# Forming two sums of the up projection's weights by adding transfers instead of beforehand on VectorE

## The chip, the cores and the metric

The kernel runs on one core of a Trainium2 chip. The core has TensorE (PE in the profile; PEld is its weight load), VectorE (DVE), ScalarE (ACT), GpSimd (POOL), and SyncE (SP), which in this kernel issues all DMA transfers; sixteen DMA engines move the data. The metric is the device time of one execution in microseconds, taken as the median over runs. All data are float32, and the answer has to agree with the float32 reference.

## The reference

One layer of a decoder. A sequence of 1024 positions with 1024 features goes through two token mixers, whose results are gated and merged, and then through a gated MLP with a short convolution:

```python
h = rmsnorm(x, mix_norm)
q, k, v, su, sv, g_a, g_b = split(h @ w_in)
y_att = sliding_window_attention(q, k, v, ...)       # window 128
y_sgu = chunked_spatial_gating(su, sv, ...)          # chunks of 128
merged = sigmoid(g_a) * (y_att @ w_oa) + sigmoid(g_b) * (y_sgu @ w_ob)
x = x + merged @ w_out

z = rmsnorm(x, ffn_norm) @ w_up                      # 1024 -> 2 * 2816
zc = conv_b + sum(conv_w[t] * shifted(z, 2 - t) for t in range(3))
gate, val = split(zc)
x = x + (silu(gate) * val) @ w_down                  # 2816 -> 1024
```

The change concerns `@ w_up`, and with it the signs of a few intermediate sums in the gate projections (`g_a`, `g_b`).

## The kernel before

**Splitting.** TensorE multiplies in a reduced float32 format (fp32r). So each operand is split into a high part (a copy by ACT into fp32r) and a low part (the original minus the high part, by POOL or DVE), and each product is made of three matmuls: high with high, high with low, low with high. A weight operand can be used only when both parts are there.

**Seven products for eight.** The gate projections and the up projection compute two output tiles of 128 rows at once (a "pair") by a Strassen-Winograd scheme: the weights and the activations of a pair are cut into 2 x 2 blocks, sums of blocks are formed, and seven block products take the place of eight. In `Blocks.prod` each product is 4 x 3 = 12 matmuls of 128x512. The weight operands are A11 and A12 (one load, `sp`, held as `lp`), A21 and A22 (one load, `sq`), and four sums: S1 = A21 + A22, S2 = S1 - A11, S3 = A11 - A21, S4 = A12 - S2. On the activation side there are B11, B21, B22 and the sums T1 to T4. The results of the products are added up in PSUM and SBUF by DVE with the signs that belong to the scheme.

**The stages in time.** Attention and the first projections run until about 180 us; then the gates (8 pairs, `gate_pair`), the branches (16 jobs of `branch`, the products with `w_oa` and `w_ob`), eight output tiles (`out_tile`, the product with `w_out`), the up stage (22 pairs: `first_pair`, then `fast_pair` for n = 1 to 21), and the down products (`mms`, lines 1661 to 1674). The order of the instructions on each engine is written out by hand: an engine runs its own instructions in program order, and waits in that order.

**The sums S1 and S3 of the up stage.** They are made ahead of their use. `sums_step` runs 22 times, twice in each gate pair from the third on and then among the branches. Each time it issues the loads of A11, A21 and A22 for a later pair (`sums_load`, tile `ls`, two buffers), lets DVE form S3 and S1 (line 620), and stores both in DRAM (`sum`). In the up stage `load_s3` and `load_q` load them again, one pair ahead: S3 into the tile `s`, and S1 together with a plain load of A22 into `lq`.

**One pair of the up stage.** While TensorE runs the products of pair n in the order A11, S3, A12, S1, A22, S2, S4, the other engines prepare pair n+1. On POOL the order is: the low part of S3 (`split_s3`), the low part of A11/A12 (`split_p`, written `pl`), S2 and S4 (`sums_r`, written `lr`), the low part of S1/A22 (`split_q`, `ql`), and the low part of S2/S4 (`split_r`, `AX`). ACT makes the high parts just before. SP issues the stores of the previous pair's activations, then the load of `lp` for pair n+2, and, in the next pair, `lq` and `s`. DVE convolves and gates the previous pair and adds up the products.

**The transition.** The weights of pair 0 are loaded by `first_left`, during output tile 4, and split during the last output tiles. Pair 1 is loaded in `first_pair`. Because the norm of the MLP's input is known only when all output tiles are there, `first_pair` also computes it (`ssq_cols`, with a power on POOL at line 129, and `rms_rows`), and T2 and T4 are split late, on DVE (`late_split`).

Of the kernel before, what the change touches and what calls it, by code (L numbers as in the profile page):

```python
# [41 lines left out]
def body(ctx, tc, nc, a):  # L42
# [579 lines left out]

    def x_gain(r, ks):
        for k in ks:
            x = xr_raw[r][:, k, :]
            nc.scalar.activation(x, x, AF.Copy, scale=cp[:, 186 + 4 * r + k:187 + 4 * r + k])

    def x_sums(ks, first):
        for k in ks:
            x0 = xr_raw[0][:, k, :]  # L630
            if first:
                sub(nc.vector, x0[:, L], x0[:, H], x0[:, L])
            else:
                x1 = xr_raw[1][:, k, :]
                sub(nc.vector, x0[:, H], x1[:, H], x0[:, H])
                sub(nc.vector, x1[:, H], x1[:, H], x0[:, L])
                sub(nc.vector, x1[:, L], x1[:, L], x1[:, H])
# [181 lines left out]
    def v_end():  # L819
# [53 lines left out]
        sums_load()  # L873
# [11 lines left out]
        nc.vector.tensor_tensor(x7, x7, e, op=ALU.add)  # L885
        nc.vector.tensor_tensor(q.g1, x5, q.g1, op=ALU.add)
        nc.vector.tensor_tensor(q.v1, x7, q.v1, op=ALU.add)
        nc.vector.tensor_tensor(q.v0, q.u2, q.v0, op=ALU.add)
# [39 lines left out]
    class Left:  # L928
# [8 lines left out]
        def load_q(self):  # L937
            if self.i is None:
                self.q = wload(self.sq, "lq")
                return  # L940
            self.q = raw("lq")
            nc.sync.dma_start(self.q[:, 0:4], pools["sum"][self.i][:, 1])
            nc.sync.dma_start(self.q[:, 4:8], self.sq[:, 4:8])

        def load_s3(self):
            self.s3 = pools["wx"].tile([128, 4, 128], F, tag="s3", name=nm("s3"))
            nc.sync.dma_start(self.s3, pools["sum"][self.i][:, 0])
# [9 lines left out]
        def sum_s3(self):  # L957
            self.s3 = s3_pool.tile([128, 4, 128], F, tag="s3", name=nm("s3"))
            sub(nc.gpsimd, self.s3, self.p[:, 0:4], self.q[:, 0:4])

        def sum_f3(self):

            sub(nc.gpsimd, self.p[:, 0:4], self.q[:, 4:8], self.r[:, 0:4])
# [15 lines left out]
        def sum_s2(self):  # L979
            self.r = raw("lr")  # L980
            sub(nc.gpsimd, self.r[:, 0:4], self.q[:, 0:4], self.p[:, 0:4])

        def sum_s4(self):
            sub(nc.gpsimd, self.r[:, 4:8], self.p[:, 4:8], self.r[:, 0:4])
# [26 lines left out]
    class Blocks:  # L1011
# [23 lines left out]
        def sums(self, x1, x7, m4):  # L1035
# [3 lines left out]
            nc.vector.tensor_tensor(self.v0, self.u2, m4, op=ALU.add)  # L1039
            nc.vector.tensor_tensor(self.v1, x7, self.v1, op=ALU.add)  # L1040
# [8 lines left out]

    sums = {"load": 0, "make": 0}  # L1050

    def sums_load():

        i = sums["load"]
        if i < NPAIR:
            x = pools["ls"].tile([128, 3, 4, 128], F, tag="ls", name=nm("ls"), bufs=2)
            nc.sync.dma_start(x[:, 0], a["wup"][2 * i][:, 0:4])
            nc.sync.dma_start(x[:, 1:3], a["wup"][2 * i + 1].rearrange("p (b k) m -> p b k m", b=2))
            sums[i] = x
            sums["load"] += 1  # L1060

    def sums_step():

        i = sums["make"]
        if i < NPAIR:
            sums_load()
            x = sums.pop(i)
            sub(nc.vector, x[:, 0], x[:, 0], x[:, 1])
            sub(nc.vector, x[:, 1], x[:, 1], x[:, 2], ALU.add)
            t = pools["dr"].tile([128, 2, 4, 128], F, tag=f"sum{i}", name=f"sum{i}")  # L1070
            nc.sync.dma_start(t, x[:, 0:2])
            pools.setdefault("sum", {})[i] = t
            sums["make"] += 1

# [27 lines left out]
    def gate_pair(c, prev):  # L1102
# [16 lines left out]
        if c > 1:  # L1119
            sums_step()  # L1120
# [12 lines left out]
        nc.vector.tensor_tensor(x7, x7, q.g1, op=ALU.add)  # L1133
        if nx:
            nx.sums_r()
        if c > 1:
            sums_step()
# [58 lines left out]
    def branch(n):  # L1196
        br, c = B_ORDER[n]

        def main(w):
# [14 lines left out]
            if n % 2 == 0 or n in (5, 9):  # L1214
                sums_step()
# [50 lines left out]
    def out_tile(i):  # L1266
        d = D_ORDER[i]

        def main(w):
# [5 lines left out]
            if i == 5:  # L1275
                lefts[0].split_s3()
# [13 lines left out]
            if d < 4:  # L1290
                eng = nc.gpsimd if i < 6 else nc.vector
                right_split("B11", k, h[:, L], eng)
                sub(nc.vector, h[:, L], h[:, H], h[:, L])
                right_split("T1", k, h[:, L], eng)
            else:
                g = hs_[k]
                sub(nc.vector, g[:, H], h[:, H], g[:, H])
# [548 lines left out]
```

## Time and profile before

| | |
|---|---|
| median of 3 runs | 1193.8 us (1193.12 to 1194.03) |
| the profiled execution | 1193.8 us, of which 1192.1 us from the first to the last instruction |
| granted TensorE clock | 1.000 |
| TensorE matmul busy | 1180.0 us, 99% of the span |
| VectorE, ScalarE, GpSimd busy | 877.8, 541.8, 567.4 us |
| moved by DMA | 191.27 MB, 160 GB/s on the mean |

A row of a group or of a timeline names the line of the kernel, the engine, the operation, what is written and read by the program's names (`out<-in`), the shapes and the count; in a timeline the start and the length in us come first, and the idle time of the engine ahead of it, with what ended it, last. `SPq` marks SP's issue of a transfer; the issue rows give the size and the time from issue to landing. A busy TensorE in the profile is not TensorE at its peak, since the matmuls overlap and their ends are modelled, so the pace is read from the starts of the matmuls in the chain of waits. The idle time of an engine that nothing waits for costs nothing.

### The profile page before, as it was taken

Reading aid. Unit: us, or ns where it says so; the run is one execution under the profiler, and the core shown is the slowest. Engines: PE = TensorE matmul, PEld = TensorE weight load, DVE = VectorE, ACT = ScalarE, POOL = GpSimd, SP = SyncE. Lnnn points to the kernel's source line nnn. Section 1 sums busy time; section 2 is a strip of 40 time slices with the busy share of each in tenths; the row PEclk is TensorE's granted clock in tenths of the full one; section 3 lists DMA queues with packets and bytes.
Section 4 is the critical chain, followed back from the end, with each engine's and each line's share of the span. In section 5 each row is a group of like instructions: output and inputs, shape, how many; then the busy total and the mean of one; then the engine's idle time right before and its main releaser. Section 6 shows DMA issues by size and latency. Waiting matters only on the chain.

```text
span 1192.1 us, 15888 instructions
## 1 busy us (share of the span) xinstructions
PE 1180.0 (99%) x5890; PEld 1000.9 (84%) x5890; DVE 877.8 (74%) x1028; ACT 541.8 (45%) x832; POOL 567.4 (48%) x364
## 2 busy tenths in 40 slices
PE   8999999999999999999999999999999999999998
PEld 8989989988888888888888888888888888888887
DVE  7798975745638565668897788878788798865674
ACT  8555567644335222234544444444444445434331
POOL 2367685487768222343756575656657551000000
PEclk9999999999999999999999999999999999999999
DMA  7110133037786997342143342423333258966471
GB/s 272 35 54 19 54 136 130 5 130 260 245 315 212 347 327 278 125 165 100 54 142 108 104 143 98 148 91 124 108 131 124 89 209 290 373 230 194 151 233 67
DMA packets 79134, 191.27 MB, mean 160 GB/s; under 512 B 8913, under 2 KB 9169, under 8 KB 79057
## 3 DMA queue, kind: packets, MB, share of 16 engines
q1 hardware_dynamic: 79056, 190.26, 45.9%
q8 instruction: 46, 0.75, 0.3%
q14 instruction: 32, 0.25, 0.1%
HBM read 139.63 MB, written 50.59 MB: 160 GB/s over the span
## 4 chain that ended last, share of the span: by engine, by line
PE 89%; DVE 4%; POOL 1%; issue 1%; ACT 0%; POOLq 0%; DVEq 0%; ACTq 0%
PE pz L1028 48%; PE pd L1672 10%; PE pdy L1672 8%; PE px L93 2%; PE px L92 2%; PE po L93 2%; PE po L92 2%; PE po L91 2%; PE px L91 2%; PE pvs L91 1%; PE pvs L92 1%; PE pvs L93 1%; DVE ya L529 1%; PE pq L91 1%; PE pq L93 1%; PE pq L92 1%
## 5 line engine op out<-in xcount | busy, mean ns | idle before, releaser
L1028 PE MATMUL pz<-T,qh 128*128 128x512 f32 x472 | 145.6, 390 | 0.0
L988 POOL TENSOR_TENSOR pl<-lp,ph 128x1024 fp32r<-128x1024 f32 x30 | 72.5, 2418 | 83.5 <-ACT ph L87 83.3
L1028 PE MATMUL pz<-B,ph 128*128 128x512 f32 x352 | 109.1, 391 | 0.0
L1028 PEld LDWEIGHTS pz<-T,qh 128*128 128x128 f32 x472 | 88.5, 188 | 18.6 <-ACT u L879 0.3
L1028 PE MATMUL pz<-T,ql 128*128 128x512 f32 x236 | 91.8, 389 | 0.0
L108 POOL TENSOR_TENSOR wjl<-wj,wjh 128x512 fp32r<-128x512 f32 (+1 forms) x24 | 40.6, 1692 | 95.8 <-ACT wjh L87 95.8
L988 POOL TENSOR_TENSOR ql<-lq,qh 128x1024 fp32r<-128x1024 f32 x30 | 76.9, 2565 | 9.1 <-ACT qh L87 9.1
L1028 PEld LDWEIGHTS pz<-B,ph 128*128 128x128 f32 x352 | 65.3, 188 | 15.0 <-ACT x L1519 1.8
L1044 DVE TENSOR_TENSOR pz<-pz,rstd_b 128x1024 f32<-128x1024 f32 x60 | 73.9, 1232 | 4.2 <-ACT rstd_b L141 2.1
L988 POOL TENSOR_TENSOR s3l<-s,s3h 128x512 fp32r<-128x512 f32 x29 | 39.8, 1373 | 69.7 <-ACT s3h L87 69.7
L1028 PE MATMUL pz<-T,s3h 128*128 128x512 f32 x232 | 71.4, 389 | 0.0
L1028 PE MATMUL pz<-B,pl 128*128 128x512 f32 x176 | 68.6, 390 | 0.0
L1672 PE MATMUL pd<-bl,ah 128*128 128x512 f32 x176 | 68.5, 389 | 0.0
L1672 PE MATMUL pd<-bh,ah 128*128 128x512 f32 x176 | 68.5, 389 | 0.0
L1672 PE MATMUL pd<-bh,al 128*128 128x512 f32 x176 | 68.5, 389 | 0.0
L1028 PE MATMUL pz<-T,AX 128*128 128x512 f32 x264 | 63.4, 389 | 0.0
L1028 PE MATMUL pz<-B,AX 128*128 128x512 f32 x264 | 63.4, 389 | 0.0
L1028 PEld LDWEIGHTS pz<-T,AX 128*128 128x128 f32 x264 | 49.6, 188 | 10.3
L1028 PEld LDWEIGHTS pz<-B,AX 128*128 128x128 f32 x264 | 49.6, 188 | 10.3
L1378 DVE SCALAR_TENSOR_TENSOR tg<-pz,cp,tg 128x1023 f32<-128x1023 f32 (+1 forms) x44 | 56.2, 1278 | 0.8
L1378 DVE SCALAR_TENSOR_TENSOR tv<-pz,cp,tv 128x1023 f32<-128x1023 f32 (+1 forms) x44 | 56.2, 1277 | 0.8
L988 POOL TENSOR_TENSOR AX<-lr,AX 128x1024 fp32r<-128x1024 f32 x22 | 53.7, 2440 | 5.1 <-ACT AX L87 5.1
(342 smaller groups left out, 3511.8 us busy)
## 6 DMA issues: line engine op xcount, KB each, us to landing
ls<-wup SPq DMA_DIRECT2D x22, 512.0 KB, 5.3
sum<-ls SPq DMA_DIRECT2D x22, 512.0 KB, 5.3
lp<-wup SPq DMA_DIRECT2D x22, 512.0 KB, 3.6
ra<-wdown SPq DMA_DIRECT2D x44, 256.0 KB, 4.6
b<-T SPq DMA_DIRECT2D x44, 256.0 KB, 3.8
B<-tv SPq DMA_DIRECT2D x33, 256.0 KB, 2.0
T<-tt SPq DMA_DIRECT2D x33, 256.0 KB, 2.0
b<-B SPq DMA_DIRECT2D x33, 256.0 KB, 3.1
```

Of the source, the lines that this page charges most:

```text
L91: nc.tensor.matmul(out, wh, mh, start=first, stop=False, **kw)
L92: nc.tensor.matmul(out, wh, ml, start=False, stop=False, **kw)
L93: nc.tensor.matmul(out, wl, mh, start=False, stop=last, **kw)
L108: nc.gpsimd.tensor_tensor(l[:, :nk, :], r[:, :nk, :], h[:, :nk, :].bitcast(F), op=ALU.subtract)
L529: nc.vector.tensor_tensor(ya[r, 2 * half:2 * half + 2, b * 128:(b + 1) * 128], p[r, g], o[r], op=ALU.add)
L988: nc.gpsimd.tensor_tensor(l, r, h.bitcast(F), op=ALU.subtract)
L1028: nc.tensor.matmul(o, p[:, k, :], y[:, q, k, :], start=not more and k == 0 and j == 0, stop=k == 3 and j == 2, skip_group_check=True)
L1044: nc.vector.tensor_tensor(z, z, rstd_b, op=ALU.mult)
L1378: nc.vector.scalar_tensor_tensor(t[:, j:], p[:, 0:1024 - j], cw[:, ci, 2 - j:3 - j], t[:, j:], op0=ALU.mult, op1=ALU.add)
L1672: nc.tensor.matmul(o[d], p[:, k - k0, m], q[:, k - k0, :], start=new and k == 0 and j == 0, stop=k == HK - 1 and j == 2, skip_group_check= ...
```

## The change

S1 and S3 of the up stage are no longer made in gates and branches. Instead, three pairs ahead, plain loads bring A11's half of `sp` into a tile for S3 and the whole of `sq` (A21, A22) into a tile for S1/A22; both lie in a new buffer `lq` with two places, in memory that the output stage has used. A pair later POOL issues two transfers that add to what lies in SBUF: A21 onto A11, which gives S3, and A22 onto A21, which gives S1. The first two pairs use the old tiles (`raw` and `s3`), with the additions issued at output tile 5 for pair 0 and in `first_pair` for pair 1. An adding transfer can only add, so S3 is now A11 + A21, and with it S2 = S1 + A11 and S4 = A12 + S2: the blocks of the scheme get other signs, and the activation sums (`x_sums`, `out_tile`, `last_tile`) and the sums of the products (`v_end`, `gate_pair`, `Blocks.sums`, `first_pair`, `fast_pair`) follow. Where the negated sum of two blocks is needed, `neg_sum` makes it in one DVE instruction. In `first_pair` the split of S3 for pair 1 comes later, behind `ssq_cols`. Everything of `sums_load` and `sums_step` is removed, with the calls in `v_end`, `gate_pair` and `branch`.

```diff
+    def neg_sum(out, x, y):
+        nc.vector.scalar_tensor_tensor(out, x, -1.0, y, op0=ALU.mult, op1=ALU.subtract)
+        return out
...
         def load_q(self):
-            if self.i is None:
-                self.q = wload(self.sq, "lq")
-                return
-            self.q = raw("lq")
-            nc.sync.dma_start(self.q[:, 0:4], pools["sum"][self.i][:, 1])
-            nc.sync.dma_start(self.q[:, 4:8], self.sq[:, 4:8])
+            self.q = wload(self.sq, "lq")
 
         def load_s3(self):
             self.s3 = pools["wx"].tile([128, 4, 128], F, tag="s3", name=nm("s3"))
-            nc.sync.dma_start(self.s3, pools["sum"][self.i][:, 0])
+            nc.sync.dma_start(self.s3, self.sp[:, 0:4])
+
+        def load_ahead(self):
+            if "lq" not in pools:
+                pools["lq"] = U("lq", F, (128, 2, 2048))
+            x = pools["lq"][:, self.i % 2, :]
+            self.s3, self.q = (x[:, i:j].rearrange("p (k m) -> p k m", m=128) for i, j in ((0, 512), (512, 1536)))
+            nc.sync.dma_start(self.s3, self.sp[:, 0:4])
+            nc.sync.dma_start(self.q, self.sq)
+
+        def adds(self):
+            nc.gpsimd.dma_start(self.s3, self.sq[:, 0:4], accum_op=ALU.add)
+            nc.gpsimd.dma_start(self.q[:, 0:4], self.sq[:, 4:8], accum_op=ALU.add)
...
-    def sums_load():
-    def sums_step():
...
# gate_pair (twice), branch, v_end
-            sums_step()
-        sums_load()
...
# out_tile
             if i == 5:
+                lefts[0].adds()
+            if i == 6:
                 lefts[0].split_s3()
...
# first_pair
         nc.scalar.copy(x7, q.v0)
+        nx.adds()
         nx.split_p()
-        nx.split_s3()
...
         ratio = ssq_cols(pb)
+        nx.split_s3()
         nx.sums_r()
         nx.split_q()
         lefts[2].load_p()
+        lefts[2].load_ahead()
...
# fast_pair
         q.prod(q.g0, "A11", "B11")
-        if nx:
-            nx.load_q()
-            nx.load_s3()
-        else:
+        if rms:
+            lefts[3].load_ahead()
+        if not nx:
             hooks[2]()
...
             lefts[n].split_r(n)
+            nx.adds()
...
         if nx:
             nx.split_s3()
+        if n + 2 < NPAIR:
+            lefts[n + 2].adds()
...
             nx.split_q()
             nx.split_r(n + 1)
+            if n + 3 < NPAIR:
+                lefts[n + 3].load_ahead()
```

More of the change, by code (lines that the diff above doesn't have):

```diff
@@ L1431, in body @@
     U_ORDER = [i for j in range(HK) for i in (j, j + HK)]
-    lefts = [Left(a["wup"][2 * i], a["wup"][2 * i + 1], i) for i in U_ORDER]
+    lefts = [Left(a["wup"][2 * i], a["wup"][2 * i + 1], n) for n, i in enumerate(U_ORDER)]
     def first_left():
@@ L1543, in fast_pair @@
             nx.split_p()
-        nc.vector.tensor_tensor(x7, x7, q.g1, op=ALU.add)
+        sub(nc.vector, x7, x7, q.g1)
         if rms:
```

71 lines of the change are left out of this document (24 added, 47 removed).

## The prediction

> **What bounds the kernel now.** I read the page first: the engines' busy time, and the chain of work that ended last.
>
> ```profile
> span 1192.1 us, 15888 instructions
> ...
> PE 1180.0 (99%) x5890; PEld 1000.9 (84%) x5890; DVE 877.8 (74%) x1028; ACT 541.8 (45%) x832; POOL 567.4 (48%) x364
> ...
> PE 89%; DVE 4%; POOL 1%; issue 1%; ACT 0%; POOLq 0%; DVEq 0%; ACTq 0%
> ```
>
> TensorE is busy for 1180.0 of 1192.1 us and carries 89% of the chain, so the change can only act through gaps that it closes or opens on TensorE. A matmul's end is modelled in such a profile, so I checked that "busy" is dense. Next view: busy time by stage (gates 245 to 415, branches 415 to 480, output tiles and first pair to 580, the other pairs to 978, the down products to the end). Then, in one fence each, the waits of TensorE from 180 us on, and two long pieces of the chain of waits (start, length, what).
>
> ```profile
> 245.00:415.00 170.00, 170.00 (x752) 140.74 (x751) 96.52 (x100) 67.26 (x83) 119.75 (x68) 1.00 0.71 246
> 415.00:480.00 65.00, 65.00 (x288) 53.86 (x287) 38.56 (x37) 14.61 (x17) 15.86 (x12) 1.00 0.81 291
> 480.00:580.00 100.00, 100.00 (x457) 83.32 (x456) 75.91 (x68) 37.23 (x50) 45.20 (x24) 1.00 0.33 117
> 580.00:978.00 398.00, 398.00 (x1756) 328.37 (x1755) 329.38 (x315) 181.79 (x212) 241.65 (x123) 1.00 0.36 122
> 978.00:1192.00 214.00, 209.91 (x926) 173.13 (x924) 146.41 (x143) 82.16 (x92) 7.55 (x4) 1.00 0.64 220
> ```
>
> ```profile
> engine line waited for: us in total, times, longest us
> ```
>
> ```profile
> 580.39 397.86 PE pz L1028 x1752
> 978.24 29.92 PE pd L1672 x132
> ```
>
> The columns after each stretch are its length, then busy us and instruction count of TensorE matmul, weight load, DVE, ACT and POOL, the granted clock, the DMA share and GB/s. TensorE fills every stage that the change touches, at a clock of 1.00, and the list of its waits from 180 us on is empty under its header. The chain gives the pace: 397.86/1752 = 227.1 ns a matmul in the up pairs, 29.92/132 = 226.7 in the down products, though the DMA share is 0.36 in the first and 0.64 in the second; in the gates, at 0.71, it is 170.00/752 = 226.1 with one matmul counted at each edge. Lighter DMA traffic buys no faster matmuls. If all of the up pairs ran at 226.7, they would lose 1752 x 0.4 ns = 0.7 us, and the gates by the same reckoning 0.3 us: 1.0 us is nearly all that can be won behind 180 us. Ahead of 180 us the change touches no instruction but the order of operands in a few subtractions.
>
> **What goes away.** Each of the 22 pairs loses its preparation in gates and branches: two loads, two DVE additions, one store, and two loads of the stored sums.
>
> ```profile
> ls<-wup SPq DMA_DIRECT2D x22, 512.0 KB, 5.3
> sum<-ls SPq DMA_DIRECT2D x22, 512.0 KB, 5.3
> ...
> ls<-wup SPq DMA_DIRECT2D x22, 256.0 KB, 4.3
> s<-sum SPq DMA_DIRECT2D x22, 256.0 KB, 3.8
> ```
>
> ```profile
> L620 DVE TENSOR_TENSOR ls<-ls 128x512 f32<-128x512 f32 x44 | 44.5, 1010 | 9.4 <-DMA ls<-wup 8.6
> ```
>
> That is 44.5 us of DVE work (44 x 1010 ns) and 22 x (512 + 256 + 512) KB of traffic. DVE is busy for only 96.52 of 170 us and 38.56 of 65 us there, TensorE never waits for it, and so this is worth 0. SP loses 66 issues in those two stages; nothing waited behind them on TensorE's path: 0.
>
> **What is added, in the steady pairs.** In pair n, POOL issues two adding transfers (256 KB each) for pair n+2, between the low part of S3 and the low part of the A11/A12 weights of pair n+1. Each occupies POOL for a time i and lands L after its issue began; neither is in this trace. Here are POOL's instructions in one pair, and the matmul that first reads the low weights (pl).
>
> ```profile
> 699.89 1.30 POOL L988 TENSOR_TENSOR s3l<-s,s3h 128x512 fp32r<-128x512 f32 x1 [3.75 <-ACT s3h L87]
> 704.52 2.40 POOL L988 TENSOR_TENSOR pl<-lp,ph 128x1024 fp32r<-128x1024 f32 x1 [3.33 <-ACT ph L87]
> 706.88 1.74 POOL L620 TENSOR_TENSOR lr<-lq,lp 128x512 f32<-128x512 f32 x1
> 708.70 1.28 POOL L620 TENSOR_TENSOR lr<-lp,lr 128x512 f32<-128x512 f32 x1
> 709.94 2.40 POOL L988 TENSOR_TENSOR ql<-lq,qh 128x1024 fp32r<-128x1024 f32 x1
> 712.30 2.40 POOL L988 TENSOR_TENSOR AX<-lr,AX 128x1024 fp32r<-128x1024 f32 x1
> 717.97 1.29 POOL L988 TENSOR_TENSOR s3l<-s,s3h 128x512 fp32r<-128x512 f32 x1 [3.26 <-ACT s3h L87]
> ```
>
> ```profile
> 711.43 0.39 PE L1028 MATMUL pz<-B,pl 128*128 128x512 f32 x1
> ```
>
> POOL is idle for 3.33 us just where the two issues go, and pl, done at 704.52 + 2.40 = 706.92, is read at 711.43: 4.51 us of slack. So 2i may reach 3.33 + 4.51 = 7.84 us, i = 3.9 us, before TensorE sees it. Two lighter conditions: POOL's six instructions sum to 11.52 us of a pair of 84 x 0.227 = 19.07 us, so it keeps up while 2i is under 7.55 us; and an addition has about 16 us until the next pair's ACT copy of S3 (just ahead of 717.97) reads it. The plain loads that an addition waits for are issued when the buffer is free, at the end of ql (712.34): with SP's issue and 3.8 to 5.3 us to landing they are there at about 717 to 718, while POOL gets to the addition at 719.26. If they are late by 3 us, POOL's idle time absorbs it.
>
> For i the nearest rows are SP's issue of such a transfer (0.36 us, below) and POOL's longest instruction in this stage (2.81 us, below); for L, 3.8 us (s<-sum) and 5.3 us (ls<-wup). A gain is excluded as an end, since the operation is added. I take i = 1.30 us, POOL's own instruction on tiles of this size, and L = 4.3 us, the 256 KB load under busy DMA. At every one of these values the steady pairs cost 0. The DMA engines carry it too: a pair's transfers grow by the 512 KB of the additions, at a share of 0.36.
>
> **What is added, at the first pairs.** Here there is no pair of lead, and the chain is read row by row.
>
> ```profile
> 578.06 2.81 POOL L988 TENSOR_TENSOR ql<-lq,qh 128x1024 fp32r<-128x1024 f32 x1
> 582.53 2.40 POOL L988 TENSOR_TENSOR AX<-lr,AX 128x1024 fp32r<-128x1024 f32 x1 [1.67 <-ACT AX L87]
> ```
>
> ```profile
> 585.77 0.62 ACT L87 ACTIVATE s3h<-s 128x512 fp32r<-128x512 f32 x1
> ```
>
> ```profile
> 581.81 0.36 SPq L947 DMA_DIRECT2D s<-sum  x1
> ```
>
> ```profile
> 586.15 0.39 PE L1028 MATMUL pz<-T,ql 128*128 128x512 f32 x1
> ...
> 597.03 0.39 PE L1028 MATMUL pz<-B,pl 128*128 128x512 f32 x1
> ```
>
> Pair 1's S3 split moves behind the power of the norm (line 129), so POOL's ql ends later by up to one such instruction, 1.30 us alone and 1.74 as slow as its like beside DVE: 580.87 + 1.7 = 582.6. TensorE reads it at 586.15, 3.5 us of cover. POOL had 1.67 us of idle before AX, so AX still ends at about 585.0. There the additions for pair 2 are issued, and behind them in POOL's order stand S3's low part for pair 2, the additions for pair 3, and pl of pair 2. S3's low part waits for ACT's copy (0.62 us, plus about 0.1 to hand over), which now waits for the addition to land; ACT's x7 copy, ph and tanh are queued behind that copy. So pl ends at 585.0 + max(L + 0.73, 2i) + 1.30 + 2i + 2.40. It is read at 597.03, so TensorE stalls by L + 2i - 7.6 us where that is positive. With i = 1.30 and L = 4.3 the sum is 6.9: no stall, 0.7 us to spare. At the low ends (0.36, 3.8): 4.5, no stall. At the high ends (2.81, 5.3): 10.9, a stall of 3.3 us, once. The spare is thin, because loads of pairs 2 and 3 now follow each other at about 580 us (the old third issue was at 581.81); I charge 0.4 us for that, about half the spare.
>
> By the Trainium skill, page "DMA: Bandwidth & Descriptors", section on the anatomy of a DMA on the gpsimd path, such a transfer takes about 2.0 us plus bytes over 436 GB/s. With L by that estimate, 2.6 us, and the same i, L + 2i is 5.2 and the sum is 1193.8 us; no run here shows that queue yet.
>
> A second place is the T2 operand of pair 0, whose low part DVE makes just behind POOL's AX of pair 0.
>
> ```profile
> 554.18 0.75 DVE L1327 SCALAR_TENSOR_TENSOR h<-ac,cp,rstd_b 128x512 f32<-128x512 f32 x1
> ...
> 556.95 2.60 DVE L1327 SCALAR_TENSOR_TENSOR h<-ac,cp,rstd_b 128x512 f32<-128x512 f32 x1
> ...
> 563.36 4.12 DVE L1456 TENSOR_TENSOR T<-T2f,T 128x1024 fp32r<-128x1024 f32 x2 [0.36 <-ACT T L87]
> ```
>
> ```profile
> 568.42 1.76 PE L1028 MATMUL pz<-T,AX 128*128 128x512 f32 x7
> ```
>
> The same instruction takes 0.75 us alone and 2.60 us beside a POOL instruction: they block each other. At the pace of 0.75 us for half the size, each T2 instruction needs about 1.3 us, so of the 4.12 us the first part was a wait, and POOL let go at about 565.0. Pair 1's additions now follow there. T2 is complete at 567.48, and its second half is read from about 568.42 + 7 x 0.227 = 570.0. If the issues hold up its second instruction wholly, 2 x 2.81 us, T2 is there at 565.0 + 5.6 + 1.3 = 571.9, a stall of 1.9 us; if not at all, 0. I take 0, since an issue reads no tile. The additions for pair 0 (output tile 5) have more than one tile, 48 x 0.227 = 10.9 us, until they are read: 0. The replaced subtractions keep count and size: the form with a scalar took 0.75 us against about 0.7 of its neighbours, eight times beside TensorE's work: 0.
>
> **Sum.** The profiled execution took 1193.8 us (span 1192.1 and 1.7 around it), the same as the median of the runs. 1193.8 - 0 (gates, branches) + 0 (20 steady pairs) + 0.4 (pair 2) + 0 (T2) = 1194.2 us.
>
> **Rivals.** (a) Slower, by one mechanism: the wait of pair 2's first product for pl, behind the additions on POOL. It decides from L + 2i = 10.0 us, a stall of 2.4 us; at the high ends it is 3.3 us, 1197.1 us. For it: four issues and one landing stand in a row, and several 512 KB loads share the DMA then. Against: it needs both prices near their high ends.
>
> (b) Slower, DVE starving the issues. DVE is busy for 329.38 of 398 us; if each issue had to wait out one DVE instruction of about 1.3 us (as T2's), i would be 1.30 + 1.3 = 2.6 us, L 5.6 and L + 2i 10.8: 1197.0 us. Beyond i = 3.8 us POOL itself becomes the bound; at i = 4.5 that is 1.5 us in each of 20 pairs, 1224 us. The row that speaks for it is 2.60 against 0.75 us; against it, that pair of instructions both read tiles.
>
> The Trainium skill, page "SBUF — State Buffer", section on who interferes with whom, says that DVE's two-port copy forms keep POOL from writing descriptors, and that a tensor_tensor holds only the read side. By that rule (b) would not occur in the pairs, where DVE runs no such copies; the trace has no POOL issue to test it.
>
> (c) Faster: the relieved DVE, SP and DMA close TensorE's gaps. There is 1.0 us to be had by the pace above: 1192.8 us, still within the band. For 2.4 us there is no place behind 180 us.
>
> (d) The change doesn't do what it says: SP comes late, the loads aren't ahead, and additions wait on POOL. Up to 7.84 us per pair less 2i this costs 0: 1193.8 to 1194.2 us.
>
> **Chances.** 0.2% (2.4 us) is about what a measurement of this kernel can tell from no change. My forecast, with (c) inside its band, 0.61, and (d) 0.04: within. (a) 0.18, (b) 0.06, both places a little and something in the first pairs that I haven't seen 0.05: slower, 0.29. Faster 0.06, for a cause ahead of 180 us. The likeliest case alone spans 1192.8 to 1196.2. The range goes down to 1192.6 and up to 1198.4, the high ends of both places in part (3.3 of pair 2, 1.3 of the 1.9 of T2), and leaves out the faster case and the saturated part of (b).
>
> **What would show it.** Right: no wait of TensorE from 180 us on, 22 pairs of POOL issues, TensorE at 227 ns in all stages, DVE in gates and branches down by some 44 us and the span unchanged. Step by step: i from the spacing on POOL, L from issue to landing, pl of pair 2 done ahead of its first reader, T2's two instructions near 4.1 us. Wrong: an idle stretch of TensorE at the start of pair 2 or in pair 0's S2 product, or gaps at every pair, which would make i larger than 3.8 us.

## The result and the profile after

The changed kernel takes 1196.67 us (median of 10 runs, 1195.9 to 1197.14); the kernel before, on the same chip, takes 1193.11 us (10 runs). The ratio is 1.0029, 95% interval [1.0019, 1.0038]: slower by 0.3%, some 3.5 us. That is inside the range on record, but not where most of the chance lay: the forecast was "no difference", and there is one. Two executions in this document were slow, one of early_x1 at 1474.64 us with a granted clock of 0.752 and one of early_i4 at 1213.84 us; the ratios leave them out.

First the page of the changed kernel: span, busy times, the new queue, and the shares of the chain that ended last.

```profile
span 1195.1 us, 15765 instructions
...
PE 1181.0 (99%) x5890; PEld 1000.1 (84%) x5890; DVE 834.6 (70%) x984; ACT 540.9 (45%) x832; POOL 596.7 (50%) x408
...
q1 hardware_dynamic: 66384, 161.42, 39.0%
q0 software_dynamic: 6336, 11.54, 6.5%
...
PE 85%; DVE 5%; POOL 2%; ACT 1%; issue 1%; DMA 0%; POOLq 0%; ACTq 0%; DVEq 0%
```

Everything that was to become lighter did: VectorE lost 43 us, and 17 MB of traffic are gone. Now the stages (the columns as in the prediction), and TensorE's waits from 180 us on (engine and line, what it waited for, us in total, times, longest).

```profile
245.00:415.00 170.00, 170.00 (x751) 140.79 (x751) 64.38 (x70) 67.37 (x83) 112.42 (x68) 1.00 0.39 136
415.00:480.00 65.00, 65.00 (x289) 53.83 (x288) 28.16 (x23) 14.61 (x17) 15.77 (x12) 1.00 0.42 146
580.00:978.00 398.00, 396.12 (x1740) 325.10 (x1739) 326.96 (x312) 178.90 (x209) 274.01 (x162) 1.00 0.53 148
```

```profile
PE pz L1039 <- ACT x L1518: 1.7, 1, 1.7
```

In gates and branches VectorE does 32.1 + 10.4 us less, TensorE was full there before and is full now: worth nothing, as forecast. The whole difference is in the up stage, where 1740 matmuls fit into the 398 us that held 1756. And the list of waits, which was empty, has one row: a wait of 1.7 us for ACT's x7 copy (line 1518). 1.7 is only half of 3.5, so a second loss is hidden from this list. It shows in the distances between the starts of TensorE's matmuls: 2.10 us instead of 0.23 at 588.09 us (pair 1, product A22), then 0.48 and 0.34 us at 603.69 (pair 2, first of A12) and 0.40 and 0.34 us at 623.13 (pair 3, the same place). After that only two are over 0.40: 0.44 us in pair 10 and 0.41 us in pair 18, again at A12.

Where the first comes from is in ACT's timeline of the transition, before and after.

```profile
585.77 0.62 ACT L87 ACTIVATE s3h<-s 128x512 fp32r<-128x512 f32 x1
586.29 0.57 ACT L1533 COPY x<-pz 128x512 f32<-128x512 f32 x1
586.75 1.07 ACT L87 ACTIVATE ph<-lp 128x1024 fp32r<-128x1024 f32 x1
...
592.97 1.06 ACT L87 ACTIVATE AX<-lr 128x1024 fp32r<-128x1024 f32 x1 [0.74 <-POOL lr L620]
596.48 0.59 ACT L1038 COPY u<-pz 128x512 f32<-128x512 f32 x1 [2.45 <-DVE pz L1037]
```

```profile
589.03 0.63 ACT L87 ACTIVATE s3h<-lq 128x512 fp32r<-128x512 f32 x1 [3.27 <-DMA lq<-wup]
589.57 0.57 ACT L1518 COPY x<-pz 128x512 f32<-128x512 f32 x1
590.03 1.06 ACT L87 ACTIVATE ph<-lp 128x1024 fp32r<-128x1024 f32 x1
...
598.14 1.06 ACT L87 ACTIVATE AX<-lr 128x1024 fp32r<-128x1024 f32 x1 [4.01 <-POOL lr L620]
599.10 0.57 ACT L1049 COPY u<-pz 128x512 f32<-128x512 f32 x1
```

ACT's copy of S3 for pair 2 now waits 3.27 us for the landing of an adding transfer. Behind it on ACT stands the x7 copy, which empties the PSUM tile into which A22 of pair 1 goes on adding: that is TensorE's wait. Behind that stands ph, and at the end of this row of work the copy AX of S2 and S4, 5.17 us later than before, and right behind it the u copy. Before, the u copy waited 2.45 us for VectorE after AX was done; that spare is eaten, and the u copy is 2.62 us late. (These are differences of the times in the two traces. Just ahead of this stretch the changed kernel is 0.1 us early, so its lateness is 0.1 us more when it is counted from there, as in the table of the next section.) On POOL the same stretch shows what stands between ph and AX.

```profile
587.90 2.41 POOL L988 TENSOR_TENSOR pl<-lp,ph 128x1024 fp32r<-128x1024 f32 x1
590.27 1.28 POOL L620 TENSOR_TENSOR lr<-lq,lp 128x512 f32<-128x512 f32 x1
591.63 1.30 POOL L620 TENSOR_TENSOR lr<-lp,lr 128x512 f32<-128x512 f32 x1
```

```profile
584.77 0.90 POOL L957 DMA_DIRECT2D lq<-wup  x1
585.86 0.85 POOL L958 DMA_DIRECT2D lq<-wup  x1 [0.18 <-issue]
589.74 1.28 POOL L999 TENSOR_TENSOR s3l<-lq,s3h 128x512 fp32r<-128x512 f32 x1 [3.04 <-ACT s3h L87]
590.98 0.85 POOL L957 DMA_DIRECT2D lq<-wup  x1
591.56 1.16 POOL L958 DMA_DIRECT2D lq<-wup  x1
592.13 3.03 POOL L999 TENSOR_TENSOR pl<-lp,ph 128x1024 fp32r<-128x1024 f32 x1
594.51 1.89 POOL L620 TENSOR_TENSOR lr<-lq,lp 128x512 f32<-128x512 f32 x1
596.48 1.63 POOL L620 TENSOR_TENSOR lr<-lp,lr 128x512 f32<-128x512 f32 x1
```

The first fence is before, the second after. The low part of S3 starts 3.04 us late, two more issues follow it, and the second sum, which AX reads, ends at 598.11 instead of 592.93. Of these 5.2 us, 4.2 are there when pl starts; most of the rest is the two sums themselves, which take 1.89 and 1.63 us instead of 1.28 and 1.30.

From the u copy on, VectorE and ACT go through a fixed row of steps in each pair (u copy, taps, x1 copy, convolution, x7 copy, and so on), and TensorE's A12 needs the PSUM tile that the x1 copy empties. In both kernels the x1 copies of a pair and of the next but one lie 38.17 us apart, while TensorE needs 168 x 0.2267 = 38.09 us for two pairs. So this second chain doesn't catch up: it was 2.61 us late at pair 2 and is 2.62 us late at pair 8. The period alone doesn't tell whether the chain could go no faster or only follows TensorE; the experiments have to.

### The profile page after: what moved, and what is told of

The parts are those of the page before. It is cut to its first block, busy times and chain, and to the rows that moved or that the text cites. A ratio compares the mean times of both kernels' runs of the same rounds, so it can differ in the third digit from the quotient of the medians.

```text
span 1195.1 us, 15765 instructions
## 1 busy us (share of the span) xinstructions
PE 1181.0 (99%) x5890; PEld 1000.1 (84%) x5890; DVE 834.6 (70%) x984; ACT 540.9 (45%) x832; POOL 596.7 (50%) x408
## 3 DMA queue, kind: packets, MB, share of 16 engines
q1 hardware_dynamic: 66384, 161.42, 39.0%
q0 software_dynamic: 6336, 11.54, 6.5%
## 4 chain that ended last, share of the span: by engine, by line
PE 85%; DVE 5%; POOL 2%; ACT 1%; issue 1%; DMA 0%; POOLq 0%; ACTq 0%; DVEq 0%
PE pz L1039 43%; PE pd L1659 10%; PE pdy L1659 8%; PE px L92 2%; PE po L93 2%; PE po L92 2%; PE px L93 2%; PE px L91 2%; PE po L91 2%; PE pvs L92 1%; PE pvs L91 1%; PE pvs L93 1%; PE pu L93 1%; PE pu L91 1%; PE pu L92 1%
## 5 line engine op out<-in xcount | busy, mean ns | idle before, releaser
L999 POOL TENSOR_TENSOR s3l<-lq,s3h 128x512 fp32r<-128x512 f32 x20 | 25.9, 1296 | 63.0 <-ACT s3h L87 63.0
L87 ACT ACTIVATE AX<-lr 128x1024 fp32r<-128x1024 f32 x22 | 23.4, 1063 | 71.0 <-POOL lr L620 71.0
```

Of the source, the lines that this page charges most:

```text
L87: return nc.scalar.activation(dst, src, AF.Copy, scale=scale)
L999: nc.gpsimd.tensor_tensor(l, r, h.bitcast(F), op=ALU.subtract)
```

## The experiments

All runs are put into one table. The first numbers are the ratio to the kernel before with its 95% interval, and the difference of the medians to the kernel before in the same comparison. The last two are worked out from the one profiled execution: the stages ahead of the up stage vary by up to 1.5 us between executions, so both are taken from a common point, a matmul of pair 0 that starts 0.324 us ahead of the next in every trace (572.86 us in the kernel before), and compared with the same distance there. One is the end of the x1 copy of pair 2, the other the start of the last matmul.

| kernel | ratio, 95% interval | median, us | x1 copy, pair 2 | last matmul |
|---|---|---|---|---|
| the change | 1.0029 [1.0019, 1.0038] | +3.56 | +2.71 | +3.38 |
| no_add2 | 0.9991 [0.9982, 1.0000] | -1.01 | -0.74 | -0.55 |
| early | 1.0001 [0.9992, 1.0009] | -0.12 | -0.71 | +1.00 |
| x7_first | 1.0029 [1.0019, 1.0038] | +3.15 | +3.15 | +4.13 |
| adds3_late | 1.0014 [1.0006, 1.0023] | +1.43 | +1.59 | +2.35 |
| both_gates | 1.0012 [1.0004, 1.0021] | +1.78 | +1.40 | +2.01 |
| act_delay | 1.0031 [1.0020, 1.0043] | +3.91 | +0.03 | +4.07 |
| act_delay3 | 1.0014 [1.0005, 1.0023] | +1.79 | +0.03 | +1.85 |
| early_i4 | 1.0068 [1.0045, 1.0091] | +8.37 | -0.73 | +3.33 |
| early_i8 | 1.0480 [1.0463, 1.0497] | +56.7 | -0.73 | +57.55 |
| before_x1 | 0.9996 [0.9987, 1.0005] | -0.61 | -1.42 | -0.34 |
| early_x1 | 0.9998 [0.9989, 1.0007] | -0.03 | -1.41 | +0.95 |
| after_x1 | 1.0039 [1.0027, 1.0052] | +5.19 | +0.75 | +6.20 |

### Is it pair 2's additions alone?

no_add2, in `fast_pair` for pair 1:

```diff
             lefts[n].split_r(n)
-            nx.adds()
```

> The changed kernel without the two additions for pair 2 (its S3 and S1 stay A11 and A21, so this part of the computation is left out); all other additions stay. Theory: the whole loss comes from pair 1, where ACT's copy of S3 waits for pair 2's addition to land and POOL runs late behind it. Then TensorE's wait of 1.7 us at pair 1's A22 is gone, ACT's u copy of pair 1 is back within 0.5 us of the kernel before, and the time is 1193.1 to 1194.1 us. Rival: the POOL issues or the added DMA traffic cost something in each of the 20 steady pairs; then at least 1.5 us of the 3.6 us stay, 1194.6 us or more.

early, the same additions issued in `first_pair`, ahead of pair 1's norm, with the loads that they need:

```diff
         nx.load_s3()
+        lefts[2].load_ahead()
...
-        lefts[2].load_ahead()
...
         nx.adds()
         nx.split_p()
+        lefts[2].adds()
...
             lefts[n].split_r(n)
-            nx.adds()
```

> The changed kernel, with pair 2's plain loads issued in the first pair just behind those of pair 1, and its additions on POOL behind the low part of pair 1's A11/A12. All additions stay. Theory: the addition lands at about 577 us, ahead of ACT's copy of S3 (585.8), POOL's later work is no longer late, and the time is that of the kernel before, 1192.9 to 1194.1 us. Rival (issues and traffic cost something in every pair): 1194.6 us or more.

Without the two additions of one pair, whose products then use unsummed blocks, the loss is gone (1192.43 us, below the 1193.1 us that were expected at the least), and issued earlier, with all 44 additions in place, it is gone too (1193.32 us). So the other 42 additions, those of the steady pairs among them, cost no more than the interval of early leaves open, about 1 us in all, and the loss is the place of two.

no_add2 also shows that the second chain has a pace of its own. There the x1 copy of pair 2 is early and TensorE's list has no wait in the up stage: up to pair 17 its A12 products start 38.08 us apart for two pairs, but the x1 copies still end 38.16 to 38.21 us apart, and the time from the x1 copy to the product that needs its tile shrinks from 1.26 us in pair 2 to 0.44 us in pair 20. A chain that only followed TensorE would keep that distance.

In early the x1 copy of pair 2 is even 0.71 us ahead of before, but the last matmul is 1.00 us behind. The wait is at the start of the down products; TensorE's wait first, then ACT's row in early, then in before.

```profile
PE pdy L1659 <- ACT pdy L1686: 0.7, 1, 0.7
```

```profile
1004.72 1.06 ACT L87 ACTIVATE ah<-ra 128x1024 fp32r<-128x1024 f32 x1 [6.80 <-DMA ra<-wdown]
...
1006.64 2.28 ACT L1686 COPY pdy<-pd 128x512 f32<-128x512 f32 x4
```

```profile
1004.81 1.06 ACT L87 ACTIVATE ah<-ra 128x1024 fp32r<-128x1024 f32 x1 [7.02 <-DMA ra<-wdown]
...
1006.73 2.27 ACT L1699 COPY pdy<-pd 128x512 f32<-128x512 f32 x4
```

The copy that TensorE waits for stands behind a high part of W_down (`ah`), which waits for a load. Counted from the common point, TensorE starts the down products 0.12 us later in early than before, so the lead of the x1 copy was used up within the up stage. The load is issued 0.15 us later than before, but takes 5.83 instead of 4.98 us to land, and TensorE loses 0.85 us. In the other traces of the table, early_i8 apart, the same load takes 4.3 to 5.6 us, in no order of the kernels. So the 1.00 us is mostly of this one execution, and says nothing of the additions; the median of early is that of the kernel before.

### Which wait of pair 1 sets the end?

x7_first, for pair 1 only, lets the x7 copy go ahead of S3's split on ACT, so that A22 has its tile in time:

```diff
+        if rms:
+            nc.scalar.copy(x7, q.v0)
         if nx:
             nx.split_s3()
         if n + 2 < NPAIR:
             lefts[n + 2].adds()
-        nc.scalar.copy(x7, q.v0)
         if not rms:
+            nc.scalar.copy(x7, q.v0)
```

> The changed kernel, with ACT's x7 copy of pair 1 ahead of its copy of S3, so that nothing that TensorE's A22 needs is queued behind the landing. POOL's order is unchanged and so is its lateness. Rival: the wait at A22 (1.87 us) is the loss, and with it gone the time falls by about 1.9 us, to 1194.8 us. Theory: DVE and ACT form a second chain with no slack, delayed by 2.6 us at pair 1's u copy (behind ACT's copy of AX, behind POOL's sums); then the wait at A22 disappears, waits at A12 of pairs 2 and 3 grow by as much, and the time stays within 0.7 us of the changed kernel, 1196.0 to 1196.9 us.

adds3_late, for pair 1 only, issues pair 3's additions behind the sums instead of ahead of pl:

```diff
-        if n + 2 < NPAIR:
+        if n + 2 < NPAIR and not rms:
             lefts[n + 2].adds()
...
         if nx:
             nx.sums_r()
+        if rms:
+            lefts[n + 2].adds()
```

> The changed kernel, with the two additions for pair 3 issued on POOL behind the sums S2 and S4 of pair 2 and no longer ahead of the low part of A11/A12. POOL's sums then end some 1.2 to 1.5 us earlier, and so does the u copy of pair 1; the wait at A22 stays at 1.87 us. Theory (loss is the larger of the wait at A22 and the lateness of the u copy): 0.5 to 0.8 us less than the changed kernel, 1195.9 to 1196.2 us. Rival (A22 alone): no difference, 1196.7 us.

Taking away TensorE's only listed wait bought nothing: x7_first takes 1196.59 us. The longer of its two waits from 180 us on (the other, 0.5 us, lies at 219 us and is also in before_x1), and behind it the rows in ACT's timeline that did it:

```profile
PE pz L1039 <- ACT x L1501: 2.5, 1, 2.5
```

```profile
588.77 0.64 ACT L87 ACTIVATE s3h<-lq 128x512 fp32r<-128x512 f32 x1 [3.05 <-DMA lq<-wup]
...
597.91 1.07 ACT L87 ACTIVATE AX<-lr 128x1024 fp32r<-128x1024 f32 x1 [5.65 <-POOL lr L620]
598.88 0.56 ACT L1049 COPY u<-pz 128x512 f32<-128x512 f32 x1
```

The wait at A22 has moved to A12 of pair 2 and become longer, 2.5 us: there TensorE meets the late x1 copy (line 1501). adds3_late is the reverse. TensorE still waits at A22, 2.1 us, yet the time falls by 1.8 us against the change, more than the 0.5 to 0.8 us that were expected, because the issues stood on the path that decides:

```profile
590.85 2.42 POOL L999 TENSOR_TENSOR pl<-lp,ph 128x1024 fp32r<-128x1024 f32 x1
593.22 1.30 POOL L620 TENSOR_TENSOR lr<-lq,lp 128x512 f32<-128x512 f32 x1
594.60 1.62 POOL L620 TENSOR_TENSOR lr<-lp,lr 128x512 f32<-128x512 f32 x1
596.17 0.86 POOL L957 DMA_DIRECT2D lq<-wup  x1
```

The second sum ends at 596.22 us in its trace and at 598.11 in that of the change, and the u copy starts at 597.22 and 599.10. But the common point is 0.75 us earlier in adds3_late, so two issues are worth 1.1 us of the chain, as the x1 copy shows too (+1.59 instead of +2.71). With that TensorE's own wait is the later one: it loses 2.4 us at A22, and its last matmul is 2.35 us behind.

both_gates makes both edits together:

> The changed kernel with both repairs of pair 1 together: its x7 copy stands ahead of the S3 split on ACT (as in x7_first), and pair 3's additions are issued behind pair 2's sums on POOL (as in adds3_late). Theory, as it stands after the runs so far: two chains run side by side, TensorE's products and the ACT-DVE-POOL chain (AX copy, u copy, tap and convolution, x1 copy), and the later one sets the end; their delays are not added. adds3_late delayed the chain by 0.74 us and TensorE by 2.4 us at A22. With both repairs TensorE waits for nothing at A22 but follows the chain from pair 2 on: x1 copy of pair 2 0.7 to 0.8 us later than before, first product of A12 of pairs 2 and 3 late by the same, end 0.75 to 1.6 us later than before, 1194.0 to 1194.9, hardly better than adds3_late (1194.87). Rival: the wait at A22 and the delay of the chain add up, so that taking both away leaves nothing: 1192.4 to 1193.2.

It takes 1195.28 us, 0.4 us above the theory's upper end and as adds3_late within the intervals; the rival, that the two delays add up, asked for 1192.4 to 1193.2 us. TensorE has no wait left at A22, but loses 0.93 + 0.11 us at A12 of pair 2 and smaller pieces behind. What remains is S3's copy on ACT, which still waits 3.08 us for the landing and holds up ph. So the end follows the later of two chains. In six of the kernels of the table with no pause placed in the stage (the change, no_add2, x7_first, adds3_late, both_gates, and early up to the down products) the last matmul is behind, or ahead, by what the x1 copy of pair 2 was, plus 0.2 to 1.0 us. Part of this surplus are two steps of about 0.3 us each, between the x1 copies of pairs 9 and 10 and of pairs 17 and 18, in all of these but no_add2. Both begin in ACT's activation of the gate half (`pz<-tg`), which starts 0.37 to 0.39 us after VectorE's last tap in pairs 9 and 17 of these five kernels and 0.09 us after it in their other pairs from the second on; in no_add2 and before it is 0.09 us throughout. Why stays open.

### Does a delay of that chain pass through to the end?

act_delay puts five copies of scratch ahead of the u copy of pair 6 in the kernel before:

```diff
         q.prod(q.v1, "S2", "T2")
+        if n == 6:
+            for _ in range(5):
+                nc.scalar.copy(q.u2, x1)
         q.sums(x1, x7, q.v0)
```

> The kernel before, with five extra copies of 128x512 on ACT in pair 6 (scratch, overwritten by the u copy that follows), about 2.6 us of work just ahead of that u copy. ACT is busy for less than half of this stage. Theory: DVE and ACT form a chain with no slack against TensorE; the delay passes through to TensorE (a wait of about 2.5 us at A12 of pair 7) and the time rises by 2.2 to 2.7 us. Rival: TensorE alone is the bound and the others have slack; the time rises by less than 0.5 us.

act_delay3 has `range(3)`:

> The kernel before, with three copies of scratch on ACT ahead of the u copy of pair 6 instead of the five of act_delay. There the five took 3.2 us, TensorE's next product began 3.2 us after the one ahead of it, and eight products then followed at 0.427 instead of 0.227 us, 1.6 us more, with a granted clock of 0.57 in that stretch; in the changed kernel and in the others with an interval of up to 2.9 us no such slow products followed. Theory: a delay of the chain passes through, and the slow products belong to the length of TensorE's pause. Three copies take 1.9 us, TensorE's interval is 1.9 to 2.2 us, no slow products follow, and the time is 1.3 to 2.1 us over that of before, 1194.6 to 1195.4 (the first number less the 0.5 us that before loses later at A12 and this one wouldn't). Rival, the slow products follow any pause at this place: 1196.2 to 1197.

Both pass through, and the chain makes up nothing in the 15 pairs that follow: the x1 copy of pair 7 is late by 3.05 us and stays so. But act_delay cost 3.9 us, more than forecast. The reason is in the stretch behind TensorE's pause; the same 4 us in act_delay and in act_delay3:

```profile
700.00:704.00 4.00, 4.00 (x11) 3.17 (x12) 3.93 (x4) 2.16 (x3) 1.29 (x1) 0.57 0.02 4
```

```profile
700.00:704.00 4.00, 4.00 (x18) 3.31 (x19) 3.93 (x4) 2.21 (x3) 1.30 (x1) 1.00 0.02 4
```

After 3.2 us from one start to the next the granted clock was 0.57 and 11 matmuls went through instead of 18: eight of them at 0.427 us, 8 x 0.2 = 1.6 us lost beside the pause itself. After 1.9 us there was nothing of the kind, and act_delay3 came out at its forecast (1195.29 us for 1194.6 to 1195.4). Nor was there after the 2.1 us of the changed kernel, so this is no part of its loss.

### How much room for issues is there in a steady pair?

early_i4 and early_i8 are early with each addition of pairs 4 and up cut into two (s = 2) or four (s = 1) pieces:

```diff
-            nc.gpsimd.dma_start(self.s3, self.sq[:, 0:4], accum_op=ALU.add)
-            nc.gpsimd.dma_start(self.q[:, 0:4], self.sq[:, 4:8], accum_op=ALU.add)
+            for k in range(0, 4, s):
+                nc.gpsimd.dma_start(self.s3[:, k : k + s], self.sq[:, k : k + s], accum_op=ALU.add)
+            for k in range(0, 4, s):
+                nc.gpsimd.dma_start(self.q[:, k : k + s], self.sq[:, 4 + k : 4 + k + s], accum_op=ALU.add)
```

> The kernel of the run early (pair 2's additions moved to where they are hidden), with every addition of pairs 4 and up issued as two halves: four issues for each pair instead of two, the same bytes. In the changed kernel's steady pairs two issues take about 1.8 us on POOL, and POOL then still waits about 2.4 us for ACT's ph before it forms pl (47.0 us in 19 pairs). Theory: the room for issues ends where that wait ends, at 1.8 + 2.4 = 4.2 us for a pair, because pl, the sums of S2 and S4, the AX copy and the u copy follow each other without slack. Four issues of 0.6 to 1.0 us each are 2.4 to 4.0 us, just inside: 1193.3 +- 0.6, as early (1193.32). Rival, an issue is paid by its descriptors rather than by its count, so that halves cost no more than the whole: 1193.3 too, with POOL's waits for ph as long as before (2.4 us).

> As early_i4, but every addition of pairs 4 and up in four quarters: eight issues for each pair, the same bytes. It tests the slack that the prediction counted: 3.33 us of POOL idle ahead of the additions and 4.51 us behind them, 7.84 us in all for two additions. Theory: only the wait for ph behind the issues is room, about 2.4 us beyond the 1.8 us that two issues take, 4.2 us; eight issues of 0.6 to 1.0 us are 4.8 to 8.0 us, so 0.6 to 3.8 us of each of some 16 to 18 pairs pass into the chain pl - sums - AX copy - u copy, 10 to 65 us in all: 1203 to 1258. Rival (the prediction's slack of 7.84 us): hidden, 1193 to 1194.5. Rival, descriptors set the cost, not issues: also hidden, 1193.3, and POOL's waits for ph stay at 2.4 us.

Eight issues cost 57 us (1250.2 us), as the theory had it; four were a miss: forecast 1193.3 us with 0.6 us allowed, measured 1201.87 us, and from 1195.8 to 1213.8 us in single runs. Its trace is of the fastest run, so it doesn't show where the others lost more. Here is one steady pair on POOL, in early and in early_i8, and then POOL's waits in the up stage of the two that name pl.

```profile
660.48 0.85 POOL L957 DMA_DIRECT2D lq<-wup  x1
661.08 1.16 POOL L958 DMA_DIRECT2D lq<-wup  x1
664.58 2.41 POOL L999 TENSOR_TENSOR pl<-lp,ph 128x1024 fp32r<-128x1024 f32 x1 [2.35 <-ACT ph L87]
```

```profile
757.39 2.62 POOL L959 DMA_DIRECT2D lq<-wup  x3
...
763.33 1.75 POOL L961 DMA_DIRECT2D lq<-wup  x2 [0.38 <-issue]
764.76 2.74 POOL L1002 TENSOR_TENSOR pl<-lp,ph 128x1024 fp32r<-128x1024 f32 x1
```

```profile
POOL pl L999 <- ACT ph L87: 46.9, 19, 4.1
```

```profile
POOL pl L1002 <- ACT ph L87: 4.1, 1, 4.1
```

In early the issues begin at 660.48 and pl at 664.58: 4.10 us of room, of which two issues use 1.76 us. In early_i8 the eight take from 757.39 to 765.08, 7.69 us, and pl no longer waits for ACT but for POOL's own issues. The overshoot is 7.69 - 4.10 = 3.6 us in a pair; measured are 57.5 us in 18 pairs, 3.2 us each. In early_i4 four took 4.0 us (662.96 to 666.97) and pl's waits for ph are gone likewise: no spare is left there, and in that fastest execution the x1 copy falls behind at two places, by 2.5 and 1.1 us.

### Can the order of the second chain be bettered?

In before_x1, early_x1 and after_x1 the x1 copy goes ahead of the tap of the value half on ACT, in all pairs from the second on:

```diff
             prev.last_sum()
-            prev.tap_v()
...
         nc.scalar.copy(x1, q.g0)
+        if not rms:
+            prev.tap_v()
```

> The kernel before, with ACT's x1 copy (which TensorE's A12 waits for) ahead of the tap of the previous pair's values in ACT's order; in the traces the product it copies is ready about 0.9 us before that tap can start. Theory: the small gaps at A12 in every second pair (about 0.5 us in all) close and the time falls by 0.3 to 0.8 us, to 1192.3 to 1192.8 us. Rival: the tap is delayed and DVE with it, no gain or up to 1 us slower.

> The changed kernel with pair 2's loads and additions earlier and the x1 copy ahead of the tap: both repairs. Theory: TensorE has no wait in the up stage at all, and the time is that of the kernel before with the reordering alone, 1192.2 to 1192.9 us, about 0.5 us under the kernel before. Rival (additions cost something per pair): 1193.5 us or more.

> The changed kernel with the same reordering of ACT (x1 copy ahead of the tap). The wait at pair 1's A22 (1.87 us) stays. Theory: with about 2 us of slack between the DVE and ACT chain and TensorE, the 0.75 us that the late u copy adds at A12 of pairs 2 and 3, and the two later losses of 0.3 us, go: 1194.8 to 1195.4 us. Rival: the losses at A12 have another cause, 1196.3 us or more.

The x1 copy is 1.4 us earlier in before_x1 and early_x1, and TensorE's small losses at A12 are gone, but in before_x1 what can be measured is nothing certain (0.9996, the interval holds 1), and in early_x1 the start of the down products takes it back as in early. after_x1 was a miss: forecast faster than the change, it takes 1198.5 us. In its trace TensorE still loses 2.0 us at A22, then 0.4 us at 900 us, and 3.8 us in pieces at the start of the down products, where its waits name VectorE's al and ACT's pdy. At 977.43 us VectorE's first al takes 3.42 us there, beside a POOL instruction that began 0.11 us ahead of it; in early_x1 the same al began 0.23 us ahead of POOL's and took 1.22 us. What stands behind it on VectorE is late by some 2 us from there on. No run tests whether this is what makes after_x1 slow, and the rest of the loss stays open. Of the kernels that compute the whole, none beats the kernel before by more than the measurement can tell.

## Why the prediction was right or wrong

**Gates, branches, VectorE, traffic: right.** 44.5 us of VectorE work went, 42.5 us of it in the two stages' rows, and TensorE's pace did not change at a DMA share of 0.39 instead of 0.71 (170.00 us hold 751 matmuls, before 752). Rival (c) had nothing to win, as argued.

**Steady pairs: the zero was nearly right, the slack behind it wrong.** Two additions cost nothing that early can show beyond some 1 us for all pairs; the two steps of 0.3 us at pairs 10 and 18 are in this stage, and whether the additions cause them is open. But the 7.84 us that two issues might take were counted to the wrong reader. I took TensorE's first matmul with pl, 4.51 us behind pl's end. There is an earlier one: POOL's sums follow pl without a gap, ACT's AX copy waits for the second sum, and the u copy stands right behind AX. In the very pair that the prediction quotes:

```profile
710.01 1.06 ACT L87 ACTIVATE AX<-lr 128x1024 fp32r<-128x1024 f32 x1 [3.39 <-POOL lr L620]
710.98 0.57 ACT L1038 COPY u<-pz 128x512 f32<-128x512 f32 x1
```

The second sum ended at 708.70 + 1.28 = 709.98; AX starts 0.03 us later and u without idle time. So the slack of pl is nought, the room is the idle time ahead of pl alone, and the bound for two issues is about 4.1 us, not 7.84. It didn't matter because two issues take 1.76 us; the 2.6 us that were taken would have fitted too. The lighter condition, that POOL keeps up while the issues are under 7.55 us, fell with it: 7.69 us cost 3.2 us in every pair, not 0.1.

**Pair 2, the step that failed.** The prediction wrote that S3's copy on ACT "now waits for the addition to land; ACT's x7 copy, ph and tanh are queued behind that copy", and then priced only one of those who wait: pl for pair 2's first product. That formula was right. It gives pl's end as 585.0 + 5.03 + 1.30 + 2.60 + 2.40 = 596.3; measured is 595.16, 3.8 us ahead of the matmul that reads it, and there was no stall. Rival (a), 1197.1 us, came near the time by a mechanism that didn't occur. The upper end of the range was made of stalls at pl and at T2, and neither occurred, so that the range holds the measured time is luck; only the chance of 0.05 for something in the first pairs that had not been seen meant such a case. The term that was missing is the same wait of 3.27 us, taken at two other readers: the x7 copy (2.0 us of TensorE at A22, shown by x7_first not to decide) and the row ph, pl, sums, AX, u copy (2.7 us after 2.45 us of spare, which decides). The charge of 0.4 us should have been about 2.7. The trace of the change is 3.4 us behind at the last matmul: the other 0.7 us was lost later, 0.6 us of it in the two steps at pairs 10 and 18, where the prediction had 0.

**"TensorE dense" was read as "the others have slack".** The chain of waits gave PE 89%, and the list of TensorE's waits was empty, so I looked for slack engine by engine. But a second chain on VectorE, ACT and POOL ran at TensorE's own pace (38.17 against 38.09 us for two pairs), hidden under starts 0.03 to 0.09 us late in every second pair from pair 7 on. So a delay in it is paid in full; act_delay3 shows 1.8 us for 1.9.

**L and i.** Taken were 4.3 and 1.30 us. From issue to ACT's release the first addition of pair 2 took 4.3 us (584.77 to 589.03); over all additions the median to landing is 5.2 us, at the upper end that was given:

```profile
lq<-wup POOLq DMA_DIRECT2D x42, 256.0 KB, 5.2
```

The estimate by the Trainium skill, page "DMA: Bandwidth & Descriptors", was 2.6 us; the median is twice that, and the measurement decides.

**Rivals (b) and (d), and T2: right to leave out.** An issue on POOL took 0.85 to 1.20 us beside a VectorE that is busy for 326.96 of 398 us; there is no starving. By the Trainium skill, page "SBUF — State Buffer", section on who interferes with whom, a tensor_tensor doesn't keep POOL from writing descriptors, and the trace agrees, as far as 0.9 us an issue can say. The second place, T2 of pair 0, shows no wait of TensorE. The loads came in time.

## What to carry to other kernels

When an operation gets a new wait, list everything that stands behind it in program order on its engine and follow each to its reader; the one priced first is not always the one that ends last. Before slack is counted on an engine off the critical path, look for the chain of its own that it belongs to, and measure how far its result comes ahead of the instruction that needs it, pair by pair. Where that distance is near nothing or shrinks, there is no slack, however empty the list of waits is. An equal period alone shows nothing, since a chain that only follows the bound engine has it too; delaying the chain on purpose settles it. An engine's idle time can take in new work only up to the next instruction that something waits for at once.

## What the runs showed of the hardware

An adding transfer, as POOL issues it here, is dear for the DMA engines. In the page's rows above, 11.54 MB of them take 6.5% of the engines' span, 11.54 MB / (0.065 x 1195.1 us) = 149 GB/s, while the plain ones make 161.42 MB / (0.39 x 1195.1 us) = 346 GB/s: 2.3 times the engine time for a byte. It isn't the size of the packets: those of 2 KB take an engine 217 ns on the mean in the adding transfers and 92 ns in the plain ones. No run has plain transfers on POOL's queue, so the adding and the queue aren't told apart. The share in the up stage went from 0.36 to 0.53 with only 148 instead of 122 GB/s.

TensorE's clock falls behind some pauses of 2 to 3 us, not behind all. Distances between two starts of 1.9, 2.1, 2.5 and 2.9 us (act_delay3, the change, adds3_late, x7_first) were followed by full speed, one of 3.2 us by 3.4 us at about half. In early_i8, which pauses at nearly every pair, one of 2.9 us was followed by the slow clock, and one of 2.2 us too:

```profile
911.60:915.10 3.50, 3.50 (x9) 2.78 (x10) 3.46 (x4) 2.20 (x3) 1.64 (x2) 0.52 0.00 0
```

The Trainium skill, page "TensorE: Matmul & The Clock Gate", section "What's actually happening", says that the clock is halved after an idle window of about 3.4 us, and that these windows run freely, whenever the work begins. The runs agree on the length, 8 x 0.427 = 3.4 us, and on the windows: in the clock records of early_i8 the first four slow stretches begin at 665.80, 710.18, 754.55 and 798.92 us, 13 x 3.413 us apart. They don't agree that a whole window has to be idle, since a pause of 2.2 us can't fill one. Laid on this grid, the pauses sort themselves by TensorE's busy time in a window:

| run, start and distance of the pause | TensorE busy in the windows it touches, us of 3.41 | granted clock in the next window |
|---|---|---|
| early_i8, 908.61, 2.9 us | 0.88 | 0.50 |
| early_i8, 932.06, 2.2 us | 1.64 | 0.50 |
| x7_first, 601.02, 2.9 us | 1.75, then 2.54 | 1.00 |
| act_delay3, 697.97, 1.9 us | 1.88 | 1.00 |

In the fourteen traces of this case, from 100 us to shortly before the end, ten windows have 1.64 us or less, and each is followed by half the clock; all others have 1.75 us or more, and none is. So about half a window of work kept the full clock, and where a pause lies on the grid decides as much as its length. This is read off the traces; no run was made to test it.

Cutting a transfer into pieces doesn't cut the price of an issue on POOL: 256 KB took 0.9 us, 64 KB 7.69 / 8 = 0.96 us.
